# Latent products before context products in a hybrid RWKV-7 / Mamba-2 / MoE layer, with other filler sizes around its scan

## Chip, cores and metric

The kernel runs on one core of one Trainium2 chip. The metric is the device time of one execution in microseconds (us). Runs of one kernel are summed up by their median. A second, profiled execution gives the trace from which rows are read here.

## What is computed

One trunk layer over 512 latent tokens and 256 context tokens of width 1024, in float32. All projections of the mixer come from one input matrix; both token streams go through it:

```python
pc = jnp.einsum('bld,de->ble', hc, p['w_in'])      # context, 256 rows
pl = jnp.einsum('bld,de->ble', hl, p['w_in'])      # latent, 512 rows
ya_c, ya_l = rwkv_branch(rw_c, rw_l, p, ctx_out)   # RWKV-7, two directions
yb_c, yb_l = ssm_branch(ss_c, ss_l, p, rows, ctx_out)   # Mamba-2, two directions
out_l = merge(ya_l, yb_l, gt_l, p)
...
def step(s, inp):                                  # RWKV: the state is carried from token to token
    sa = jnp.einsum('bhvk,bhk->bhv', s, -kk_t)
    s = s * w_t[:, :, None, :] + sa[..., None] * (kk_t * a_t)[:, :, None, :] + v_t[..., None] * k_t[:, :, None, :]
...
xbc = jax.nn.silu(dw_conv_centred(xbc, p['ssm_conv_w'], p['ssm_conv_b']))   # Mamba: convolution over 5 tokens
```

A mixture of 16 experts follows. The change does not touch it.

## The kernel before

**Stages.** The trace has these stretches, in us from the start of the span: normalisation and first projections up to 165; the preparation of the RWKV scan (`rw_all`) up to some 640; the RWKV scan in four passes up to 1141; the Mamba stage (`ssd_prep`, `ssd_main`) up to 1500; then the merge, the routing and the experts.

**A projected block.** `inproj_g` (L301) makes 128 output columns of `w_in`: eight k-tiles (`KT`), each with three products, since a float32 number is split into a rounded part and its rest: `whi`·`hlH`, `whi`·`hlL`, `wlo`·`hlH`. That is 24 matmuls of 512 columns into the PSUM tile `pl` for the latents (L312) and, where `ctx` holds, 24 of 256 columns into `pc` for the context (L315). The two alternate, matmul by matmul, so that both end together. The function is a generator: it yields the columns of each matmul. Both tiles come from the PSUM pool `ip` under one tag, with 4 buffers in `rw_all`, 3 in the scan and 2 in the Mamba stage (`ipb`). The weights are loaded (`wraw`), rounded by ScalarE (`whi`, L284) and subtracted by GpSimd (`wlo`, L287) a block ahead.

**Who takes the results away.** In the scan, blocks are the Mamba convolution's (`conv`, L445). ScalarE copies `pc` (L453) and `pl` (L454) into `u`, VectorE does four multiply-adds (L463), GpSimd a product (L466). Blocks of the kinds z and g (`zgate`, L471) have no context. In `rw_all`, `shift` (L319) reads `pl` and `pc`: ScalarE copies, VectorE does two multiply-adds each.

**The scan and its filler.** `scan` (L895) has 12 steps a pass, 48 in all. A step is a chain: small matmuls (`pch<-SV,sAL`), a VectorE copy to `R` (L930), small matmuls (`pch<-R,sTT`), copies to `SV` by VectorE (L944) and ScalarE (L945), small matmuls (`pch<-SV,sBT`), and a VectorE product into the next `SV` (L954). While TensorE would wait for each of the three, `self.feed(self.hop)` issues matmuls of projected blocks worth `HOP` = 3200 columns (L940, L948, L960). The sum of filler is fixed: what isn't issued in the scan is issued after it.

**After the scan.** The readout of the last pass, `rw_out` (L963), treats two heads' pairs one after the other. Each has three products into one PSUM tile `po` (a single buffer): means (L981), variances (L987) and gate (L996), with ScalarE and VectorE work between them. The loop at L2027 issues one part of it, then 3000 columns of filler, eight times; then the rest of the filler is issued (L2030). Next come 36000 columns of gate blocks (L2043, kind g), which TensorE's order places partly among the products of the readout, and the first transposes of the Mamba stage (`sps<-ident,Bc`, L1134), whose operands `Bc`, `Cc`, `xc` SyncE's queue loads (L1119 to L1124).

**Order.** On TensorE the order within a stage is that of the code. On the other engines a scheduler sets it.

Of the kernel before, what the change touches and what calls it, by code (L numbers as in the profile page):

```python
# [19 lines left out]
SEQ = 512  # L20
CTX = 256
TOK = CTX + SEQ
KT = D // 128
# [1 line left out]
ROWS = SEQ // NCOL  # L25
EPS = 1e-6

HOP = 3200
HOP3 = 2600
HOP4 = 8000  # L30
PREPC = 7500
# [56 lines left out]
class Block:  # L88
# [212 lines left out]
    def inproj_g(self, n, ctx, w):  # L301


        nc = self.nc
        hi, lo = w
        pl = self.ip.tile([128, SEQ], F32, name="pl", tag="ip", bufs=self.ipb)
        pc = self.ip.tile([128, CTX], F32, name="pc", tag="ip", bufs=self.ipb) if ctx else None
        for j, (w_, H) in enumerate(((hi, 0), (hi, 1), (lo, 0))):
            x = (self.hlL, self.hcL) if H else (self.hlH, self.hcH)
            for kt in range(KT):  # L310
                e = dict(start=j + kt == 0, stop=j == 2 and kt == KT - 1)
                nc.tensor.matmul(pl[:n], w_[:, kt, :n], x[0][:, kt, :], **e)  # L312
                yield SEQ
                if ctx:
                    nc.tensor.matmul(pc[:n], w_[:, kt, :n], x[1][:, kt, :], **e)  # L315
                    yield CTX
        return pl, pc

    def shift(self, dst, off, pl, pc, blk):  # L319
# [1626 lines left out]
def body(tc, A, out):  # L1946
    with ExitStack() as ctx:
        B = Block(tc, A, out)
# [22 lines left out]
        pl = lambda n, **k: tc.tile_pool(name=n, bufs=1, reuse_waits="tile", **k)  # L1971
# [4 lines left out]
        with ExitStack() as hx:  # L1976
# [22 lines left out]
            with pl("ip", space=PSUM) as B.ip, pl("sc") as sc, pl("scp", space=PSUM) as scp, ExitStack() as scx:  # L1999
                B.zeros(sc)  # L2000
                B.setup_conv(sc, ("u", "acc", "sg"))
                B.fill, B.credit = B.filler(sc, B.blocks), 0
                B.hop = HOP
                side = B.rw_last(scp)
                with tc.manual_schedule(engines={mybir.EngineType.PE}):
                    for p in range(4):
                        py = B.scan(sc, scp, p, side)
                        if p == 0:
                            for _ in side:
                                B.feed(SF)  # L2010
                            tpx.close()
                            rs = rsx.enter_context(pl("rs", side="right"))
                            B.sqs, B.ones = rs.tile([128, SEQ], F32, name="sqs"), rs.tile([128, 128], F32, name="ones")
                            sp = hx.enter_context(pl("ssdc", side="right"))
                            sc2 = scx.enter_context(pl("sc2"))
                            B.late = itertools.chain(B.ada_late(sc2, 0), B.ada_late(sc2, 1))
                        side = B.rw_out(sc2, scp, p, py)
                        next(side)
                        if p == 1:
                            setup = B.ssd_setup(sp, sc2, scp)  # L2020
                            next(setup)
                            next(setup)
                        elif p == 2:
                            next(setup)
                            next(setup)
                            next(setup, None)
                    for _ in range(8):  # L2027
                        next(side, None)
                        B.feed(3000)
                    B.feed(1 << 30)  # L2030
                    B.fill = B.filler(None, [("g", b) for b in range(G1, 16)])
                    next(B.fill)
# [75 lines left out]
```

## Time and profile before

| | us |
|---|---|
| median of three runs | 2183.39 (2180.47 to 2185.78) |
| the profiled execution | 2184.98 |
| its span from first to last instruction | 2183.1 |
| TensorE busy in it | 1923.5 (88%) |
| VectorE, ScalarE, GpSimd busy | 1171.0, 847.5, 634.0 |

A matmul's duration in the trace holds its way through the array, and successive matmuls overlap: the time that a matmul costs in a row of them is the distance of starts, not the duration. Idle time of an engine counts only where something later waits for that engine.

### The profile page before, as it was taken

How to read it: one execution, taken by the hardware profiler on the slowest of the kernel's cores; microseconds unless marked ns; L12 is line 12 of the kernel's file. 1: busy time of each engine (PE TensorE's matmuls, PEld its weight loads, DVE VectorE, ACT ScalarE, POOL GpSimd, SP SyncE). 2: the span in 40 equal slices, each digit the busy share in tenths (PEclk: the TensorE clock that was granted, in tenths of full speed). 3: DMA queues.
4: the chain of work that ended last, by engine and by line, in shares of the span. 5: the costliest groups of instructions: out<-in, count | busy, mean ns of one | idle time of the engine just before them, and what ended most of it. 6: DMA issues, size and time to landing. Idle time of an engine off the chain costs nothing. (4 is left out here: it accounts for less than half of the span.)

```text
span 2183.1 us, 35294 instructions
## 1 busy us (share of the span) xinstructions
PE 1923.5 (88%) x13996; PEld 1270.6 (58%) x14016; DVE 1171.0 (54%) x1941; ACT 847.5 (39%) x1423; POOL 634.0 (29%) x482
## 2 busy tenths in 40 slices
PE   4979798889768887999997999789999998999997
PEld 2756566566646665666775665467887453433332
DVE  4455987887895858444542466763455112322214
ACT  5444454455343344352535443454333121111113
POOL 2243333433241222332334475663111000000002
PEclk8989998898888999999999999989999999999999
DMA  6246679768879686886546334336866898999997
GB/s 234 77 110 152 158 162 196 146 169 178 183 180 244 184 255 211 286 260 192 162 125 209 113 112 143 131 132 233 279 219 265 334 369 328 409 409 409 408 409 300
DMA packets 444735, 495.16 MB, mean 227 GB/s; under 512 B 138521, under 2 KB 339471, under 8 KB 441499
## 3 DMA queue, kind: packets, MB, share of 16 engines
q1 hardware_dynamic: 419899, 449.29, 64.9%
q0 software_dynamic: 7808, 26.74, 3.4%
q10 hardware_dynamic: 16864, 16.88, 2.4%
q8 instruction: 110, 1.80, 0.3%
q14 instruction: 54, 0.44, 0.1%
HBM read 393.96 MB, written 97.98 MB: 225 GB/s over the span
## 5 line engine op out<-in xcount | busy, mean ns | idle before, releaser
L287 POOL TENSOR_TENSOR wlo<-wraw,whi 128x1024 fp32r<-128x1024 f32 x92 | 231.1, 2512 | 483.0 <-ACT whi L284 222.0
L312 PE MATMUL pl<-hlH,whi 128*128 128x512 f32 x672 | 243.1, 440 | 20.8 <-ACT zg L484 6.5
L312 PE MATMUL pl<-hlH,wlo 128*128 128x512 f32 x672 | 237.8, 431 | 0.0
L312 PE MATMUL pl<-hlL,whi 128*128 128x512 f32 x672 | 232.7, 426 | 0.0
L1705 PE MATMUL ph<-ew,xe 128*64 128x512 f32 x432 | 197.2, 599 | 2.0 <-DMA ew<-in_exp_w_dram 2.0
L1704 PE MATMUL ph<-ew,xe 128*64 128x512 f32 x432 | 196.9, 598 | 0.0
L284 ACT ACTIVATE whi<-wraw 128x1024 fp32r<-128x1024 f32 x93 | 98.1, 1055 | 220.8 <-DMA wraw<-in_w_in_dram 133.4
L312 PEld LDWEIGHTS pl<-hlH,whi 128*128 128x128 f32 x672 | 131.0, 199 | 64.4 <-issue 15.5
L312 PEld LDWEIGHTS pl<-hlL,whi 128*128 128x128 f32 x672 | 127.3, 194 | 39.9 <-issue 14.1
L312 PEld LDWEIGHTS pl<-hlH,wlo 128*128 128x128 f32 x672 | 127.8, 196 | 38.0 <-issue 13.1
L1704 PEld LDWEIGHTS ph<-ew,xe 128*64 128x64 f32 x432 | 56.6, 137 | 110.8 <-issue 109.8
L463 DVE SCALAR_TENSOR_TENSOR cacc<-u,cst,cacc 128x772 f32<-128x772 f32 (+1 forms) x96 | 97.9, 1020 | 30.9 <-ACT cacc L459 29.3
L315 PE MATMUL pc<-hcH,whi 128*128 128x256 f32 (+1 forms) x312 | 97.1, 312 | 12.8 <-ACT u L454 7.4
L1791 PE MATMUL pye<-ew,ewx 128*64 128x512 f32 x448 | 107.7, 632 | 0.0
L315 PE MATMUL pc<-hcH,wlo 128*128 128x256 f32 (+1 forms) x312 | 96.6, 313 | 0.0
L315 PE MATMUL pc<-hcL,whi 128*128 128x256 f32 (+1 forms) x312 | 95.6, 310 | 0.0
L1214 ACT ACTIVATE M<-sel,ncumT 128x128 f32<-128x128 f32 x256 | 69.1, 386 | 66.3 <-PE sel L1211 66.2
L1711 ACT ACTIVATE ewx<-ph 128x512 f32<-128x512 f32 x30 | 17.9, 598 | 187.3 <-PE ph L1705 173.8
L1819 DVE TENSOR_TENSOR macc<-macc,psc 128x512 f32<-128x512 f32 x56 | 37.7, 685 | 93.2 <-PE psc L1814 93.1
L466 POOL TENSOR_TENSOR cacc<-cacc,csg 128x772 f32<-128x772 f32 (+1 forms) x24 | 42.9, 1788 | 146.4 <-ACT csg L465 145.8
L1215 DVE TENSOR_TENSOR M<-M,cb 128x512 f32<-128x512 f32 x64 | 63.0, 996 | 34.6 <-ACT M L1214 34.5
L1870 POOL TENSOR_TENSOR macc<-macc,x 128x512 f32<-128x512 f32 x7 | 11.4, 1653 | 227.8 <-DVE macc L1869 226.5
(575 smaller groups left out, 4265.7 us busy)
## 6 DMA issues: line engine op xcount, KB each, us to landing
ew<-in_exp_w_dram SPq DMA_DIRECT2D x126, 1024.0 KB
ew<-in_exp_w_dram SPq DMA_DIRECT2D x90, 512.0 KB
wraw<-in_w_in_dram SPq DMA_DIRECT2D x83, 512.0 KB
adaw<-in_ada_w_dram SPq DMA_DIRECT2D x24, 1024.0 KB
cst<-in_exp_w_dram SPq DMA_DIRECT2D x14, 1024.0 KB
BTd<-BT ACTq DMA_DIRECT2D x48, 256.0 KB
sAL<-ALd SPq DMA_DIRECT2D x23, 512.0 KB
sBT<-BTd SPq DMA_DIRECT2D x23, 512.0 KB
```

Of the source, the lines that this page charges most:

```text
L284: pin(nc.scalar.activation(hi, raw, AF.Copy))
L287: self.lo.tensor_sub(lo, raw, hi.bitcast(F32))
L312: nc.tensor.matmul(pl[:n], w_[:, kt, :n], x[0][:, kt, :], **e)
L315: nc.tensor.matmul(pc[:n], w_[:, kt, :n], x[1][:, kt, :], **e)
L463: e.scalar_tensor_tensor(acc[:, s0:s0 + n0], u[:, s0 + k:s0 + k + n0], cw[:, b, k:k + 1], acc[:, s0:s0 + n0], op0=OP.mult, op1=OP.add)
L466: nc.gpsimd.tensor_mul(acc[:, s:s + n], acc[:, s:s + n], sg[:, s:s + n])
L1214: nc.scalar.activation(M[:, c], pt[:, c * 128:c * 128 + 128], AF.Exp, bias=self.ncumT[:, c, r:r + 1])
L1215: nc.vector.tensor_mul(M.rearrange("p c t -> p (c t)"), M.rearrange("p c t -> p (c t)"), cb)
L1704: nc.tensor.matmul(ph[e][f][0:64], x, w1[j][:, fs], start=kt == 0, stop=kt == 7, skip_group_check=True)
L1705: nc.tensor.matmul(ph[e][f][64:128], x, w3[j][:, fs], start=kt == 0, stop=kt == 7, skip_group_check=True)
L1791: nc.tensor.matmul(py[64 * c:64 * c + 64], hd[e][:, kt], w2[j][:, 512 * c:512 * c + 512], start=kt == 0, stop=kt == 7, skip_group_check=True)
L1819: nc.vector.tensor_add(a, a, pc)
```

## The change

Three edits. In `inproj_g`, all 24 latent matmuls of a block now come first, then its 24 context matmuls; the weights, the operands and the count stay. `HOP` falls from 3200 to 3000 columns. The loop after the scan feeds 8000 columns a step in place of 3000.

```diff
-HOP = 3200
+HOP = 3000
...
-        for j, (w_, H) in enumerate(((hi, 0), (hi, 1), (lo, 0))):
-            x = (self.hlL, self.hcL) if H else (self.hlH, self.hcH)
-            for kt in range(KT):
-                e = dict(start=j + kt == 0, stop=j == 2 and kt == KT - 1)
-                nc.tensor.matmul(pl[:n], w_[:, kt, :n], x[0][:, kt, :], **e)
-                yield SEQ
-                if ctx:
-                    nc.tensor.matmul(pc[:n], w_[:, kt, :n], x[1][:, kt, :], **e)
-                    yield CTX
+        for o, x, cols in ((pl, (self.hlH, self.hlL), SEQ), (pc, (self.hcH, self.hcL), CTX))[:1 + ctx]:
+            for j, (w_, h) in enumerate(((hi, 0), (hi, 1), (lo, 0))):
+                for kt in range(KT):
+                    nc.tensor.matmul(o[:n], w_[:, kt, :n], x[h][:, kt, :], start=j + kt == 0, stop=j == 2 and kt == KT - 1)
+                    yield cols
         return pl, pc
...
                     for _ in range(8):
                         next(side, None)
-                        B.feed(3000)
+                        B.feed(8000)
                     B.feed(1 << 30)
```

**Where one block ends and the next begins, in the scan.** TensorE's order in the last pass, before the change; `hl` are latent operands, `hc` context operands, and `whi` follows `wlo` where the next block begins:

```order
L315 MATMUL pc<-hcH,wlo 128x256
L312 MATMUL pl<-hlH,wlo 128x512
L315 MATMUL pc<-hcH,wlo 128x256
L312 MATMUL pl<-hlH,whi 128x512
L315 MATMUL pc<-hcH,whi 128x256
```

The same place now:

```order
L311 MATMUL pc<-hcH,wlo 128x256 x2
L311 MATMUL pl<-hlH,whi 128x512 x5
L898 MATMUL pch<-R,sTT 64x64 x8
L311 MATMUL pl<-hlH,whi 128x512 x3
L311 MATMUL pl<-hlL,whi 128x512 x3
```

The first context matmul of a block stood second in it, and now stands after its 24 latent ones.

**ScalarE at the end of the scan, before.** `u` is the convolution's input, `oy` the scan's result, `SV` a copy of the chain:

```order
L454 ACTIVATE u_6507<-pl 128x8x64
L453 ACTIVATE u_6507<-pc 128x256
L459 ACTIVATE cacc<-u_6507,cst 128x772
L945 ACTIVATE SV<-pch 64x2x128
L971 ACTIVATE oy<-py_10402 128x512
L971 ACTIVATE oy<-py_10400 128x512
```

And now:

```order
L450 ACTIVATE u_6509<-pl 128x8x64
L941 ACTIVATE SV<-pch 64x2x128
L967 ACTIVATE oy<-py_10318 128x512
L967 ACTIVATE oy<-py_10316 128x512
L284 ACTIVATE whi<-wraw 128x1024
L449 ACTIVATE u_6509<-pc 128x256
L455 ACTIVATE cacc<-u_6509,cst 128x772
```

The copy of `pl` stood directly ahead of that of `pc`; now four instructions lie between.

**TensorE after the scan, before.** From the last context matmul of the filler to the gate product of the second pair; the rows between are gate blocks:

```order
L315 MATMUL pc<-hcH,wlo 128x256
L996 MATMUL po<-cst,lg 128x512
L312 MATMUL pl<-hlH,whi 128x512 x8
L312 MATMUL pl<-hlL,whi 128x512 x8
L312 MATMUL pl<-hlH,wlo 128x512 x8
L312 MATMUL pl<-hlH,whi 128x512 x8
L312 MATMUL pl<-hlL,whi 128x512 x4
L981 MATMUL po<-oy,cst 128x512
L312 MATMUL pl<-hlL,whi 128x512 x4
L312 MATMUL pl<-hlH,wlo 128x512 x8
L987 MATMUL po<-oy,cst 128x512
L996 MATMUL po<-cst,lg 128x512
```

The second pair's three products now:

```order
L977 MATMUL po<-oy,cst 128x512
L311 MATMUL pc<-hcH,whi 128x256 x7
L311 MATMUL pc<-hcL,whi 128x256 x8
L311 MATMUL pc<-hcH,wlo 128x256 x8
L983 MATMUL po<-oy,cst 128x512
L311 MATMUL pl<-hlH,whi 128x512 x8
L311 MATMUL pl<-hlL,whi 128x512 x8
L311 MATMUL pl<-hlH,wlo 128x512 x8
L311 MATMUL pl<-hlH,whi 128x512 x2
L992 MATMUL po<-cst,lg 128x512
L311 MATMUL pl<-hlH,whi 128x512 x6
```

The filler reached to the first pair's gate product and now reaches to the second pair's variances; 26 matmuls of gate blocks stand between the second pair's last two products, where there were none. From the last small matmul of the scan to the first transpose of `Bc` there are 28416 columns more than before.

## Rows read from the trace of the kernel before

**Rows 1.** The page: busy time, share of the span, instructions.

```profile
PE 1923.5 (88%) x13996; PEld 1270.6 (58%) x14016; DVE 1171.0 (54%) x1941; ACT 847.5 (39%) x1423; POOL 634.0 (29%) x482
```

**Rows 2.** By stretch: length; busy PE, PEld, DVE, ACT, POOL; granted clock; DMA; GB/s.

```profile
165.00:703.00 538.00, 446.76 (x3810) 335.13 (x3808) 422.05 (x760) 251.99 (x372) 192.94 (x117) 0.89 0.76 175
703.00:826.90 123.90, 108.05 (x1489) 81.39 (x1489) 90.12 (x164) 45.74 (x69) 35.08 (x28) 0.98 0.77 228
...
1054.80:1140.90 86.10, 83.74 (x1002) 63.73 (x1002) 43.06 (x68) 40.62 (x53) 31.95 (x24) 1.00 0.52 156
1140.90:1182.50 41.60, 30.49 (x117) 21.97 (x117) 13.02 (x14) 22.71 (x27) 16.78 (x13) 0.88 0.54 186
```

**Rows 3.** What TensorE waited for, 703 to 1140.9 us: total, times, longest.

```profile
PE pch L902 <- DVE SV L944: 10.4, 9, 2.8
PE pc L315 <- ACT u L454: 7.4, 9, 1.0
PE pl L312 <- ACT u L454: 5.4, 5, 1.1
PE pch L902 <- DVE SV L954: 4.6, 4, 3.6
PE pch L902 <- ACT SV L945: 3.1, 6, 1.2
PE pch L902 <- DVE R L930: 2.9, 3, 2.2
```

**Rows 4.** Instructions in order of time at one block boundary in the last pass.

```profile
1117.71 0.42 DVE L930 COPY R<-pch 128x256 f32<-128x256 f32 x1 [1.85 <-PE pch L902]
...
1119.05 1.11 ACT L454 ACTIVATE u<-pl 128x512 f32<-128x512 f32 x1 [4.36 <-PE pl L312]
...
1120.21 0.39 PE L315 MATMUL pc<-hcH,whi 128*128 128x256 f32 x1 [0.85 <-ACT u L454]
...
1121.23 0.68 PE L902 MATMUL pch<-R,sTT 64*64 64x64 f32 x16
```

**Rows 5.** Line L315 alone: minimum, median, maximum in ns of one instruction.

```profile
L315 PEld LDWEIGHTS pc<-hcH,wlo x312: 134/189/337, 68.5 to 1148.5; 128*128 128x128 f32 x152, 128*64 128x64 f32 x4
L315 PE MATMUL pc<-hcH,wlo x312: 274/280/686, 68.6 to 1148.7; 128*128 128x256 f32 x152, 128*64 128x256 f32 x4
```

**Rows 6.** TensorE in order of time, in the first projections.

```profile
68.58 0.99 PE L315 MATMUL pc<-hcH,wlo 128*128 128x256 f32 x7
```

**Rows 7.** TensorE in order of time, after the scan.

```profile
1146.49 1.12 PE L987 MATMUL po<-oy,cst 128*128 128x512 f32 x2 [0.29 <-ACT oy L984]
...
1151.64 2.12 PE L312 MATMUL pl<-hlH,whi 128*128 128x512 f32 x8 [1.76 <-ACT u L453]
1153.60 1.99 PE L312 MATMUL pl<-hlL,whi 128*128 128x512 f32 x8
1155.42 1.98 PE L312 MATMUL pl<-hlH,wlo 128*128 128x512 f32 x8
...
1168.07 1.13 PE L996 MATMUL po<-cst,lg 128*128 128x512 f32 x2 [3.47 <-ACT osd L989]
1174.79 3.78 PE L312 MATMUL pl<-hlH,whi 128*128 128x512 f32 x8 [5.59 <-ACT zg L484]
...
1182.47 0.60 PE L1134 MATMUL sps<-ident,Bc 128*128 128x128 f32 x4
```

**Rows 8.** The same stretch on VectorE: the reading of the first gate product.

```profile
1155.65 0.67 DVE L997 TENSOR_TENSOR od<-od,po 128x512 f32<-128x512 f32 x1
```

**Rows 9.** The columns of rows 2, around the last of these waits.

```profile
1172.00:1177.00 5.00, 2.21 (x5) 1.82 (x6) 1.38 (x2) 1.11 (x2) 1.42 (x2) 0.50 1.01 369
```

**Rows 10.** SyncE's queue: the first loads of the Mamba stage.

```profile
1168.93 0.52 SPq L1119 DMA_DIRECT2D Bc<-xd  x1
```

**Rows 11.** What TensorE waited for, 165 to 703 us.

```profile
PE pbt L760 <- DVE X L741: 21.3, 12, 4.8
PE pvt L621 <- DVE v L329: 6.8, 4, 3.1
```

## Prediction

> **What bounds the kernel now.** The page comes first: TensorE is busy for 88% of the span, the next engine for 54% [rows 1]. That is a mean, so the second view is the busy time by stretch [rows 2]. In the scan's last pass (1054.8 to 1140.9) TensorE is busy for 83.7 of 86.1 us: the scan's chain of waits is covered there, and a column of filler taken out shortens the pass. In 703 to 826.9 it is 108.1 of 123.9 us while VectorE has 90.1: there the chain sometimes ends last. Right after the scan (1140.9 to 1182.5) TensorE has only 30.5 of 41.6 us, at a mean granted clock of 0.88: too little filler is left. Before 703 (`rw_all`) VectorE leads with 422.1 of 538 us, and TensorE waits.
>
> The third view is what TensorE waited for in 703 to 1140.9 [rows 3]. Two kinds must be told apart. The waits of `pch` (10.4 + 4.6 + 3.1 + 2.9 us, 22 times) belong to the scan's chain. Those of `pc` and `pl` on ScalarE's copy `u` (7.4 + 5.4 us, 14 times) belong to the filler, and their place in time [rows 4] shows why. With three PSUM buffers, `pl` and `pc` of one block hold two, the next block's `pl` takes the third, and its `pc` needs the buffer of the `pl` that has just ended. That `pl` is copied from 1119.05 on, 1.11 us long; the `pc` matmul, second in its block, stands idle for 0.85 us and starts at 1120.21.
>
> **The change part by part: the order of products.** Nothing is added or removed: each block keeps its 24 matmuls of either size and their weight loads. Once the context products come last, `pl` has been complete for 24 matmuls when its buffer is wanted, and the next block's `pl` takes a buffer that was copied a block earlier. Seven context matmuls in a row took 0.99 us [rows 6]; with the 0.28 us of one (the median of [rows 5]) that is (0.99 - 0.28) / 6 = 0.118 us from start to start, so 24 last 2.8 us against the copy's 1.11 us. All 14 waits should go: 12.8 us. What is late next? After the example the chain's next matmul starts at 1121.23, and its `R` was ready at 1117.71 + 0.42 = 1118.13 [rows 4]: 3.1 us of room. Where a chain wait follows more closely the gain is swallowed; I take off 2 us: **-10.8 us** (bounds 0, if a chain wait takes the place of each, and -15, as 0.85 us idle in the example is 1.0 us of lost starts). The copies of `pc` now end a block alone, behind other ScalarE work, which costs nothing as long as `u` has its second buffer.
>
> Does TensorE pay for the new order? Before, a latent and a context matmul with the same weights stood side by side. The row says that nothing was shared: each of 312 context matmuls of a kind has a weight load of its own, 0.189 us at the median, and at 0.118 us from start to start it is hidden even where context follows context [rows 5, 6]. I take 0. The Trainium skill, page "TensorE: Matmul & The Clock Gate", section "Part 2: What happens when you issue a matmul", speaks against the change: weights stay put, so load once and multiply repeatedly, and a load takes the columns divided by 1.2, some 107 ns for 128. By that page the change would give up a shared load for 3 x 312 = 936 matmuls, an estimate of 100 us; by the rows it gives up none.
>
> **HOP.** 46 of the 48 steps lie after 703, but all 48 get three times 200 columns less: 28800 columns. Eight latent matmuls start 1.82 us apart (1153.60 to 1155.42, [rows 7]), 0.2275 us for 512 columns, so 28800 columns are 12.8 us. An interval that now ends in a chain wait gives nothing back: 22 of 46 x 3 = 138, or 16%. **-10.7 us** (bounds 0 and -12.8). Fewer convolution blocks in the scan also take VectorE work out of it, which I don't count.
>
> **After the scan.** The 28416 columns of the new order come here: **+12.6 us**. They lie between the readout's products, and cover what is idle now [rows 7]: 0.29 us before the variances, 1.76 us on the copy of `pc`, 3.47 us on `osd`, 5.59 us on `zg`: **-11.1 us**. Before the last product runs TensorE waits 3.47 us and after it 5.59 us, and the granted clock then is 0.50 [rows 9], the lower level of 1.2 GHz: eight matmuls in 3.78 us. The 23 matmuls from 1174.79 to the transposes at 1182.47 took 7.7 us, at 0.2275 us each they take 5.2: **-2.4 us** if TensorE stays busy. New waits: the second pair's means need the single `po` buffer, which is free when VectorE has read the gate product, 1155.65 + 0.67 - 1146.49 = 9.8 us after the first pair's variances start [rows 7, 8]. In the new order two feeds (8000 columns, 3.55 us each) and two products (1.1 us each) lie between, 9.3 us, and one more rounding of weights stands in ScalarE's order ahead of that reading. I take **+3 us** of waits (bounds 0 and 8). They also hold the loads of `Bc` and `xc`: issued 13.5 us before the transposes now [rows 7, 10], one weight load earlier in SyncE's order after the change, with 45 gate-block matmuls (10.2 us) behind the last product to cover them. Sum for this stretch: +2.1 us.
>
> **`rw_all` and the rest.** `HOP` isn't used there. The order is, and it lets `shift` begin on `pl` 2.8 us earlier; VectorE's order changes with it. I take 0 between -9 and +8 (below).
>
> **Sum.** -10.8 - 10.7 + 2.1 = -19.4 us on the profiled execution's 2184.98: 2165.6. The median lies 1.6 us lower (2183.39), so I forecast **2164**.
>
> **The rivals.**
> 1. *The scan is bound by its chain.* Then neither the filler's cut nor the buffer's release shortens it, and the columns are paid for after it: +2.1 us, about 2185.5. For it: 22 chain waits, VectorE at 73% in 703 to 826.9. Against: the last pass, 97% TensorE [rows 2], and the room of 3.1 us [rows 4].
> 2. *Weight loads come to light (slower).* If a context matmul hides only 0.118 us of its 0.189 us load once 24 stand in a row, each loses 0.07 us: 936 x 0.07 = 66 us, less the gain of 19: about 2230. It decides from 0.02 us a matmul on (19.4 / 936). Against it: the seven in a row at 0.118 us. The section of the Trainium skill named above would put the loss higher still, at its estimate of 100 us.
> 3. *`rw_all` gains too.* TensorE waits 21.3 us for `X` and 6.8 us for `v` on VectorE [rows 11]. If `shift` moves out of their way and a third of it goes, 9 us: 2155.
> 4. *`rw_all` loses.* VectorE executes in order; an early `shift` that waits for its `pl` holds up the products behind it. If each of the 12 waits for `X` grows by one VectorE instruction of 512 columns, 0.67 us as in [rows 8], that is +8: 2172.
> 5. *The edits do nothing to the waits* (the scheduler moves the copies so that the buffer is late again): only `HOP` counts, -8.6: 2175.
>
> **How the numbers follow.** Likeliest 0.60, with its own range 2157 to 2171; rival 1: 0.08; 2: 0.03; 3: 0.12; 4: 0.11; 5: 0.06. The measurement tells about 0.2% (4.4 us) from no change: faster is below 2179.0. Faster: 0.60 + 0.12 + 0.11 + 0.06 less a tail of 0.03, 0.86; same: 0.08 (rival 1 and some of the tail); slower: 0.06 (rival 2, the rest). The range takes in rivals 3, 4 and 5 and the bounds of new waits: 2150 to 2179.
>
> **What the new profile would show.** Right: no waits of projected blocks' products for `u` in the scan; a last pass shorter by some 3 us; the stretch from the scan's last matmul to the first `Bc` transpose about as long as now (41.6 us), but with TensorE busy for nearly all of it at a granted clock near 1. Wrong: chain waits well over 21 us; context matmuls over 0.118 us from start to start; a wait of more than 5 us between the second pair's products or before the `Bc` transposes; a change before 703.

## The result and the profile after

The changed kernel takes **2206.5 us** (median of 4 runs, 2201.4 to 2207.1) against 2184.6 (4 runs, 2180.5 to 2189.1): a recorded ratio of 1.0092, 95% interval 1.0074 to 1.0110 (the quotient of the two medians is 1.0100). It is slower; the forecast was 2164 in 2150 to 2179. The profiled execution took 2201.42 us, span 2199.3.

The page of after: busy time, share of the span, instructions (to be set against [rows 1]).

```profile
PE 1928.4 (88%) x14016; PEld 1273.5 (58%) x14016; DVE 1166.6 (53%) x1941; ACT 851.3 (39%) x1424; POOL 629.7 (29%) x482
```

No engine was given more work, so the time went into waits and clock. What TensorE waited for in the scan of after (engine, line, releaser: total us, times, longest), to be set against [rows 3]:

```profile
PE pch L898 <- DVE SV L940: 16.1, 8, 7.2
PE px L832 <- DMA T<-d: 6.1, 1, 6.1
PE pch L898 <- DVE R L926: 5.3, 6, 1.5
PE pch L898 <- ACT SV L941: 4.3, 7, 1.5
PE py L898 <- DVE SV L940: 3.9, 1, 3.9
PE pch L898 <- DVE SV L950: 3.8, 5, 1.3
```

The waits of `pl` and `pc` for `u` are gone, as forecast. The chain's waits have grown from 21.0 us (the four rows of `pch` in [rows 3]) to 29.5 (the four rows of `pch` here).

After by stretch, columns as in [rows 2]: the last pass over the same steps, and the stretch from the scan's end to the first transpose of `Bc`.

```profile
1056.50:1140.10 83.60, 81.37 (x990) 61.34 (x989) 40.85 (x65) 39.92 (x52) 29.16 (x23) 1.00 0.52 162
1140.10:1196.20 56.10, 43.61 (x196) 34.22 (x196) 23.28 (x20) 29.46 (x36) 24.78 (x18) 0.88 0.41 136
```

The last pass is 2.5 us shorter (forecast 3). The stretch after the scan takes 56.1 us in place of 41.6, at the same granted clock of 0.88, so the idle time that the new columns were to cover is still there: 56.1 - 43.6 = 12.5 us without TensorE, 41.6 - 30.5 = 11.1 before. Where it sits now, TensorE in order of time:

```profile
1162.77 2.08 PE L977 MATMUL po<-oy,cst 128*128 128x512 f32 x2 [4.13 <-DVE od L993]
...
1189.00 3.78 PE L311 MATMUL pl<-hlH,whi 128*128 128x512 f32 x8 [8.36 <-ACT zg L480]
```

The first wait is the one for the single `po`, and its cause is on VectorE: the reading of the gate product stands behind four multiply-adds of the convolution.

```profile
1156.95 5.16 DVE L459 SCALAR_TENSOR_TENSOR cacc<-u,cst,cacc 128x772 f32<-128x772 f32 x4
1162.03 0.68 DVE L993 TENSOR_TENSOR od<-od,po 128x512 f32<-128x512 f32 x1
```

The second is a chain over several engines. The rows of ScalarE, GpSimd and SyncE's queue in after, in order of time:

```profile
1170.68 12.58 SPq L281 DMA_DIRECT2D wraw<-in_w_in_dram  x2
...
1177.30 0.86 ACT L461 ACTIVATE csg<-cacc 128x772 f32<-128x772 f32 x1 [0.92 <-DVE cacc L459]
...
1178.23 1.89 POOL L462 TENSOR_TENSOR cacc<-cacc,csg 128x772 f32<-128x772 f32 x1 [1.79 <-ACT csg L461]
1180.05 2.81 POOL L287 TENSOR_TENSOR wlo<-wraw,whi 128x1024 fp32r<-128x1024 f32 x1
...
1183.36 0.52 SPq L1115 DMA_DIRECT2D Bc<-xd  x1
...
1187.41 1.06 ACT L284 ACTIVATE whi<-wraw 128x1024 fp32r<-128x1024 f32 x1 [7.79 <-DMA wraw<-in_w_in_dram]
1188.37 0.58 ACT L480 ACTIVATE zg<-pl 128x512 f32<-128x512 f32 x1
```

GpSimd makes the last convolution's product at 1178.23, then `wlo`; the second of the two weight loads is issued only when `wlo` has freed a buffer (1182.9), ScalarE's `whi` waits for it until 1187.41, and `zg`, a copy that was ready to run since TensorE ended that block, stands behind `whi`. Eight matmuls after the wait take 3.78 us, the lower of the clock's two levels, as in [rows 7].

### The profile page after: what moved, and what is told of

It reads as the page before. It is cut to its first block, busy times and chain, and to the rows that moved or that the text cites. A ratio compares the mean times of both kernels' runs of the same rounds, so it can differ in the third digit from the quotient of the medians.

```text
span 2199.3 us, 35321 instructions
## 1 busy us (share of the span) xinstructions
PE 1928.4 (88%) x14016; PEld 1273.5 (58%) x14016; DVE 1166.6 (53%) x1941; ACT 851.3 (39%) x1424; POOL 629.7 (29%) x482
## 5 line engine op out<-in xcount | busy, mean ns | idle before, releaser
L287 POOL TENSOR_TENSOR wlo<-wraw,whi 128x1024 fp32r<-128x1024 f32 x92 | 223.2, 2426 | 507.5 <-ACT whi L284 301.7
L311 PE MATMUL pl<-hlH,whi 128*128 128x512 f32 x672 | 217.1, 443 | 17.6 <-ACT zg L480 8.4
L311 PE MATMUL pl<-hlL,whi 128*128 128x512 f32 x672 | 213.0, 437 | 0.0
L311 PE MATMUL pl<-hlH,wlo 128*128 128x512 f32 x672 | 209.1, 431 | 0.0
L311 PEld LDWEIGHTS pl<-hlH,whi 128*128 128x128 f32 x672 | 126.4, 198 | 57.4 <-issue 16.6
L311 PEld LDWEIGHTS pl<-hlH,wlo 128*128 128x128 f32 x672 | 123.6, 194 | 42.4 <-issue 17.0
L459 DVE SCALAR_TENSOR_TENSOR cacc<-u,cst,cacc 128x772 f32<-128x772 f32 (+1 forms) x96 | 105.0, 1094 | 28.2 <-ACT cacc L455 26.6
L1700 PEld LDWEIGHTS ph<-ew,xe 128*64 128x64 f32 x432 | 56.5, 137 | 109.0 <-issue 107.9
L1787 PE MATMUL pye<-ew,ewx 128*64 128x512 f32 x448 | 110.9, 647 | 0.0
L1815 DVE TENSOR_TENSOR macc<-macc,psc 128x512 f32<-128x512 f32 x56 | 37.7, 685 | 89.5 <-PE psc L1810 89.3
L1866 POOL TENSOR_TENSOR macc<-macc,x 128x512 f32<-128x512 f32 x7 | 11.4, 1654 | 229.7 <-DVE macc L1865 228.4
L1787 PEld LDWEIGHTS pye<-ew,ewx 128*64 128x64 f32 x448 | 33.2, 149 | 65.3 <-issue 64.6
L1803 DVE TENSOR_TENSOR yhl<-yf,yhl 64x512 fp32r<-64x512 f32 x30 | 20.5, 686 | 84.0 <-ACT yhl L1802 83.5
L690 POOL TENSOR_TENSOR t<-nkk,a 128x768 f32<-128x768 f32 x16 | 39.1, 2443 | 87.2 <-ACT a L659 59.3
```

The source lines that it names most:

```text
L287: self.lo.tensor_sub(lo, raw, hi.bitcast(F32))
L311: nc.tensor.matmul(o[:n], w_[:, kt, :n], x[h][:, kt, :], start=j + kt == 0, stop=j == 2 and kt == KT - 1)
L459: e.scalar_tensor_tensor(acc[:, s0:s0 + n0], u[:, s0 + k:s0 + k + n0], cw[:, b, k:k + 1], acc[:, s0:s0 + n0], op0=OP.mult, op1=OP.add)
L690: nc.gpsimd.tensor_mul(ka, nkk, a)
L1700: nc.tensor.matmul(ph[e][f][0:64], x, w1[j][:, fs], start=kt == 0, stop=kt == 7, skip_group_check=True)
L1787: nc.tensor.matmul(py[64 * c:64 * c + 64], hd[e][:, kt], w2[j][:, 512 * c:512 * c + 512], start=kt == 0, stop=kt == 7, skip_group_check=True)
```

## The experiments

All were timed in five rounds, in four groups, each on one chip beside the kernel before (medians of before 2188.6, 2186.4, 2186.8, 2185.3 us). The table cuts each profiled execution at the same instructions. Preparation: from the first pair's transposes (`pvt`) to the scan's first matmul. Start: to the zeroing of the first `py` (step 3). Passes: from one zeroing to the next, the last to its last `py<-sRB`. Tail: to the first transpose of `Bc`. Mamba: to the merge's first product. Lengths in us; one execution each, so a few us between kernels mean little.

| kernel | prep. | start | pass 1 | 2 | 3 | 4 | tail | Mamba | ratio to before [95%] |
|---|---|---|---|---|---|---|---|---|---|
| before | 562.6 | 39.5 | 122.2 | 110.9 | 115.1 | 77.2 | 41.5 | 331.3 | |
| after | 573.5 | 36.4 | 125.9 | 111.1 | 106.3 | 75.7 | 56.1 | 330.7 | 1.0092 [1.0074, 1.0110] |
| 1 order | 581.7 | 35.6 | 132.9 | 112.5 | 106.8 | 76.6 | 41.8 | 329.2 | 1.0061 [1.0037, 1.0085] |
| 2 HOP | 559.7 | 37.5 | 138.4 | 97.9 | 112.3 | 76.2 | 63.9 | 331.6 | 1.0096 [1.0063, 1.0129] |
| 3 feed | 563.0 | 38.2 | 123.0 | 113.3 | 113.0 | 77.1 | 47.8 | 331.9 | 1.0025 [1.0006, 1.0045] |
| 4 HOP, feed | 559.2 | 37.6 | 138.5 | 97.6 | 112.3 | 76.1 | 60.9 | 330.4 | 1.0096 [1.0064, 1.0128] |
| 5 order in prep. | 579.3 | 37.3 | 128.8 | 111.7 | 115.5 | 77.4 | 41.6 | 331.2 | 1.0082 [1.0056, 1.0108] |
| 6 order in scan | 565.9 | 35.5 | 129.7 | 114.8 | 105.2 | 76.8 | 41.1 | 334.4 | 0.9992 [0.9973, 1.0011] |
| 7 HOP late | 554.0 | 37.9 | 126.4 | 112.4 | 109.8 | 81.0 | 49.5 | 331.0 | 1.0061 [1.0038, 1.0085] |
| 8 after, zg on DVE | 580.1 | 32.9 | 130.2 | 113.9 | 107.9 | 75.7 | 48.8 | 341.8 | 1.0115 [1.0095, 1.0136] |
| 9 as 5, VT on DVE | 581.2 | 44.8 | 121.2 | 112.1 | 114.7 | 77.6 | 41.5 | 330.2 | 1.0061 [1.0039, 1.0082] |
| 10 as 5, not pair 8 | 572.5 | 42.3 | 121.2 | 112.5 | 115.4 | 77.4 | 41.8 | 331.0 | 1.0070 [1.0048, 1.0092] |
| 11 as 6, zg repaired | 554.2 | 36.5 | 128.9 | 112.5 | 105.2 | 76.8 | 43.0 | 325.7 | 0.9960 [0.9939, 0.9981] |
| 12 after, zg repaired | 571.3 | 33.0 | 132.9 | 111.9 | 107.7 | 75.7 | 50.0 | 333.7 | 1.0049 [1.0032, 1.0066] |
| 13 prep. by weight | 567.1 | 37.7 | 123.6 | 111.7 | 114.4 | 77.3 | 41.5 | 331.1 | 1.0028 [1.0006, 1.0050] |
| 14 before, zg repaired | 565.4 | 37.9 | 122.2 | 111.6 | 112.9 | 77.4 | 41.7 | 327.4 | 0.9970 [0.9954, 0.9985] |
| 15 HOP, zg repaired | 561.4 | 37.4 | 136.8 | 98.6 | 110.9 | 76.3 | 55.8 | 335.7 | 1.0070 [1.0048, 1.0093] |
| 16 as 11, by weight | 559.1 | 37.9 | 122.9 | 114.7 | 103.3 | 77.5 | 42.6 | 328.2 | 0.9957 [0.9941, 0.9974] |

**1 to 4: the edits apart.** One hunk of the diff each: the order of products (1), `HOP = 3000` (2), `B.feed(8000)` (3), the last two together (4).

> Latent products first, alone (HOP 3200 and feeds of 3000 as before). Theory A (the loss is made after the scan, by the columns that HOP and the 8000 put there): the stretch from the scan's last matmul to the first Bc transpose stays within 3 us of the 42.6 us of before, the waits of pl and pc for the copy u in the scan go, and the time is 8 to 12 us under the kernel before. Theory B (the order of products upsets VectorE and ScalarE in the preparation and the first pass): 5 to 13 us over the kernel before, with 5 to 8 us of it ahead of 703 us.

> HOP 3000 alone, the old order of products, feeds of 3000. Theory A: the scan is shorter by some 10 us and the stretch after it longer by 10 to 14 us, so the time is within 5 us of the kernel before. Theory B: nothing ahead of 703 us changes, the stretch after the scan takes the columns into its waits, and the time is 5 to 10 us under the kernel before.

> Feeds of 8000 columns alone. The old order leaves some 12000 columns after the scan, so two feeds take them all. Theory A: the first pair's means come up to 2.5 us later and the time is within 4 us of the kernel before. Theory B: no difference, within 4 us.

> HOP 3000 and feeds of 8000, the old order of products. Theory A: the waits of the changed kernel after the scan are here too (4 us ahead of the second pair's means, 8 us ahead of the third gate block), the stretch after the scan is 52 to 57 us, and the time is 2 to 6 us over the kernel before. Theory B: the stretch after the scan is 42 to 46 us and the time 6 to 10 us under the kernel before.

No edit gains by itself. 2, 3 and 4 are slower than either theory expected (by 21, 5 and 21 us over before), and 1 lies at or just over the upper end of theory B's range; by place, theories A (the tail) and B (the preparation and first pass) each hold a part. The order loses ahead of the tail; `HOP` loses 22 us in the tail and gives nothing in the scan (the passes sum to 425.4 before, 424.8 with it); 8000 columns lose 6 us in the tail. They do not add up: 0.6% and 1.0% apart, 0.9% together.

**5 and 6: where the order loses.** `inproj_g` takes the new loop in one stage and the old one elsewhere:

```diff
+        if self.ipb == 4:        # 5: the preparation; 6: ipb == 3, the scan
+            for o, x, cols in ((pl, ...
+        else:
+            for j, (w_, H) in enumerate(...
```

> The new order of products in the preparation of the scan alone; the scan's filler and what follows keep the old order, HOP 3200 and 3000 columns a step. Theory B (the order's loss is made in the preparation, where ScalarE copies r ahead of the weights' rounding and of VT, so that TensorE waits for VT, falls to the lower granted clock and hands a later start to the scan): the scan begins 8 to 18 us later than before, 1.004 to 1.008 times the time before (about 2198). Rival (the loss is made by the order in the scan's first pass): the scan begins within 3 us of before and the time is within 0.2%.

> The new order in the scan's filler alone; preparation in the old order, HOP 3200, 3000 columns a step. Theory B: the waits of projected blocks for u in the scan go (12.8 us in the trace of before) and nothing is lost ahead of it, so 5 to 12 us faster, 0.994 to 0.998 times the time before. Rival (the first pass loses by the order itself, as the run with the order alone lost 10.7 us there): first pass 5 to 11 us longer, time within 0.2% of before or above.

The loss is made in the preparation: 579.3 us, and in the five kernels with the new order as it is there 571 to 582 (mean 577), against 554 to 566 (mean 560) in the ten that keep the old one. In 5 the first pass is 6.6 us longer as well, though its order is the old one; 9 and 10, below, don't show that. In the scan alone (6) the order neither loses nor gains, where 5 to 12 us were expected: the rival came out, a first pass longer by 7.5 us. The scan's waits in 6:

```profile
PE pch L909 <- DVE SV L951: 15.9, 12, 5.2
PE pch L909 <- DVE R L937: 7.3, 7, 3.2
PE pch L909 <- ACT SV L952: 3.5, 6, 1.3
PE px L843 <- DMA T<-d: 3.4, 2, 2.9
PE pch L909 <- DVE SV L961: 2.1, 3, 1.3
```

12.8 us of waits for `u` are gone, and the chain's four rows of `pch` come to 28.8 us in place of 21.0 [rows 3]: 8 of 13 us are taken back by the chain. By place, the third pass is 9.9 us shorter and the first two 11.4 longer.

**7: HOP's cut in the last two passes only.**

```diff
+                        B.hop = HOP if p < 2 else 3000
                         py = B.scan(sc, scp, p, side)
```

> HOP 3200 in the first two passes and 3000 in the last two; order and the rest as before. Theory H (HOP's cut shortens a pass where TensorE is the bound, and in the first pass it only lets VectorE's dt work in ahead of the chain's copies): the first two passes within 3 us of before, the last two 3 to 6 us shorter together, the stretch after the scan 8 to 12 us longer for 14400 columns (6.4 us) and new waits: 1.001 to 1.004 times the time before. Rival (the columns are covered after the scan): that stretch at most 3 us longer, time 0.998 to 1.000.

The second pass moved by 1.5 us and the first by 4.2 (at most 3 expected), and 14400 columns cost the tail 8 us, as theory H has it; but the last two passes together gave 1.4 us in place of 3 to 6, and the ratio is above the expected 1.004. In the last pass VectorE has 42.4 us of work in place of 37.0: again work of its own came to lie elsewhere.

**8, 12, 14, 15: the wait for `zg`.** In 8 VectorE copies the first two gate blocks after the scan; the others have two `zg` buffers in the Mamba stage as well ("repaired").

```diff
-            nc.scalar.activation(t, pl, AF.Copy)
+            nc.vector.tensor_copy(t, pl) if G1 <= b - 16 < G1 + 2 else nc.scalar.activation(t, pl, AF.Copy)
...
-        t = pool.tile([128, SEQ], F32, name="zg", tag=tag, bufs=bufs)
+        t = pool.tile([128, SEQ], F32, name="zg", tag=tag, bufs=bufs or (2 if self.ipb == 2 else 1))
```

> The changed kernel, but VectorE in place of ScalarE copies the first two gate blocks after the scan (zg), so that the copy doesn't stand behind a rounding of weights. Theory C (after the scan TensorE waits 8.4 us, and then runs at the lower clock, because zg stands behind whi, which waits for a weight load): that wait goes, the stretch from the scan's end to the first Bc transpose falls from 56 to 47 to 50 us, the time from 1.009 to 1.005 to 1.006 times that of before. Rival (the loads of Bc, issued 12.8 us before the transposes, end just as late): the transposes wait for them instead, the stretch stays above 53 us and the time at 1.008 to 1.010.

The tail fell to 48.8 us, as theory C said, and the time did not fall (1.0115, where 1.005 to 1.006 was expected): the wait came back one block later, since the second copy needs the one `zg` buffer, whose store is queued behind the loads of `Bc` and `xc`. TensorE's waits in 8, from the scan's last steps into the Mamba stage:

```profile
PE pl L311 <- DVE zg L480: 8.3, 2, 7.5
PE po L977 <- DVE od L993: 4.1, 1, 4.1
```

The same view of 12, from the scan's end on:

```profile
PE po L977 <- DVE od L993: 4.1, 1, 4.1
PE sps L1136 <- DMA xc<-xd: 3.4, 4, 1.5
PE sps L1130 <- DMA Bc<-xd: 1.9, 1, 1.9
PE pl L311 <- DVE zg L480: 0.7, 1, 0.7
```

> The changed kernel with the same two repairs of zg. Theory C2: the 8.4 us wait before the transposes and the 7.5 us wait one block later, which took its place when VectorE copied zg into a single buffer, both go; the stretch from the scan's end to the first Bc transpose takes 47 to 50 us and the Mamba stage stays at 331: 1.003 to 1.006 times the time before. Rival: the loads behind it end last instead, 1.008 or more.

With two buffers both waits go, as theory C2 has it, and the changed kernel comes from 1.0092 to 1.0049. By the traces the tail gets 6.0 us shorter and the Mamba stage 3.0 longer. What ends next is there: 5.3 us for `xc` and `Bc`.

> The kernel before with only the two repairs of zg (VectorE copies the first two gate blocks after the scan; two zg buffers in the Mamba stage). If the repair made the 0.4% of the run with the scan's new order: 0.996 to 0.998. If the order made it: 0.999 to 1.001.

> HOP 3000 alone, old order, with the two repairs of zg; HOP 3000 alone was 1.0096. Theory H (the scan gives back 4 us at most for 28800 columns, and 12.6 us of them are paid after it): the repairs take off 0.3 to 0.5%, 1.0045 to 1.0065 stays. Rival (HOP fails by the waits for zg after the scan alone): 1.001 or less.

The repair gains 0.3% on the kernel before as well (14), so that little of the 0.43% in 12 is peculiar to the new tail. With it the cut of `HOP` still costs 1.0% (1.0070 of 15 over 0.9970 of 14), more than theory H expected: the passes give back 1.4 us (422.6 against 424.0), the tail takes 14.1 more, of which the columns are 12.6, and the Mamba stage 8.3. In 15 TensorE doesn't wait for `zg` in the tail at all, so `HOP`'s loss is not that wait.

**9, 10, 13: how the preparation loses.** From 5 on, 9 lets VectorE copy `VT` in the last of the eight pairs, and 10 keeps the old order in that pair; 13 sorts the products by weight part (16 latent, 16 context ones with `whi`, then 8 and 8 with `wlo`).

```diff
-            nc.scalar.activation(VT[:, i0:i0 + n], pt[:, :n], AF.Copy)
+            (nc.vector.tensor_copy(VT[:, i0:i0 + n], pt[:, :n]) if p == 7 else nc.scalar.activation(...))
```

> The new order in the preparation alone, as in the run of that (1.0082), and in the last of its eight pairs VectorE in place of ScalarE copies VT, so that VT no longer stands behind whi. In that run the last pair took 83.2 us and the scan began at 690.5. Theory V (the last pair's loss is VT standing behind a rounding of weights on ScalarE, with the lower granted clock after that wait): the last pair takes 76 to 78 us, the time is 1.004 to 1.006 times that of before. Rival (the loss is made by other work, VectorE's above all): the last pair stays at 81 us or more and the time at 1.007 or more.

> The new order in the first seven pairs of the preparation, the old one in the last pair and in all that follows; ScalarE's order around the last VT is that of before. Theory V: the last pair takes 73 to 76 us as in the kernels with the old order, and what is left is the 6 to 9 us of the first three pairs: 1.003 to 1.005 times the time before. Rival (the loss is one of the state at the start of the pair, such as VectorE running late): the last pair still takes 80 us or more, time 1.007 or more.

> In the preparation alone the products are sorted by weight part: 16 latent and 16 context products with whi, then 8 and 8 with wlo; whi is released after two thirds of a block, as before, and pl ends 8 context products (0.94 us) ahead of pc in place of 24. The rest as before. Theory W (the new order loses in the preparation because whi is held to the end of the context products, some 1.9 us longer): the preparation up to the scan's start takes within 5 us of before (676), time 1.000 to 1.003 times that of before. Rival (the early end of the latents reorders ScalarE and VectorE; the last VT still stands behind whi here): scan from 684 on, 1.005 to 1.008.

The last pair (from its `pvt` to the scan) takes 73.6 us before, 81.2 in after and 83.2 in 5; 79.0 in 9, 77.0 in 10, 75.5 in 13. ScalarE in order of time at its start, in the kernel before:

```profile
604.40 0.40 ACT L791 ACTIVATE Tf<-T 96x256 f32<-96x256 f32 x1
604.70 0.84 ACT L622 ACTIVATE VT<-pvt 128x512 f32<-128x512 f32 x2
606.22 1.06 ACT L284 ACTIVATE whi<-wraw 128x1024 fp32r<-128x1024 f32 x1 [0.67 <-DMA wraw<-in_w_in_dram]
```

The same place in after:

```profile
603.01 0.67 ACT L323 ACTIVATE r<-pl,cst 128x512 f32<-128x512 f32 x1
607.47 1.06 ACT L284 ACTIVATE whi<-wraw 128x1024 fp32r<-128x1024 f32 x1 [3.80 <-DMA wraw<-in_w_in_dram]
608.43 0.85 ACT L618 ACTIVATE VT<-pvt 128x512 f32<-128x512 f32 x2
```

`VT` now stands behind a `whi` that waits 3.80 us for its load. TensorE, in order of time, waits for `VT` and then runs at the lower of the clock's levels:

```profile
609.06 0.65 PE L652 MATMUL ra<-low,lwh 128*128 128x512 f32 x1 [2.25 <-ACT VT L618]
```

The last pair, and 20 us in it, in the view by stretch of before:

```profile
602.51:676.08 73.57, 55.46 (x544) 39.47 (x542) 71.14 (x140) 33.04 (x50) 25.79 (x16) 0.86 0.81 196
606.00:626.00 20.00, 17.59 (x123) 11.72 (x121) 19.09 (x29) 13.90 (x17) 12.36 (x7) 1.00 0.59 135
```

The same two stretches of after:

```profile
603.52:684.74 81.22, 61.66 (x545) 42.75 (x543) 71.68 (x139) 33.13 (x49) 26.02 (x16) 0.79 0.74 177
606.00:626.00 20.00, 17.75 (x105) 11.48 (x104) 15.98 (x23) 13.43 (x17) 7.15 (x4) 0.74 0.45 106
```

The same matmuls (544, 545) keep TensorE busy for 6.2 us more: most of the pair's 7.6 us is clock, and the clock falls behind a wait of 2 us. The other runs agree: in after, 1, 5, 8 and 12 TensorE waits 2.25 to 2.44 us for `VT` at this place and the granted clock falls to 0.50; in before, 9 and 13 it waits 0.44 to 1.22 us and the clock stays at 1.00 for the next 15 us and more. (In 10, at 1.78 us, it falls for some 4 us, behind a further wait.) No run changes this wait alone. 10 shows the place: with ScalarE's order of before the pair is 6 us shorter than in 5. 9 shows the mechanism in part (79.0 us against 76 to 78 expected): the clock holds behind `VT`, and falls 20 us later, behind a wait of 2.79 us for `X`.

But the ratios, 1.0061 and 1.0070, are hardly under the 1.0082 of 5, and 10's preparation is still 12 us over the mean of the old order: more than half of the loss lies in the seven pairs ahead. There, too, the waits for `VT` grow. What TensorE waited for between 165 and 680 us, the rows of `VT`, before:

```profile
PE ra L656 <- ACT VT L622: 6.5, 5, 2.2
PE rac L632 <- ACT VT L622: 3.2, 2, 2.7
```

The same in after:

```profile
PE rac L628 <- ACT VT L618: 12.0, 3, 4.3
PE ra L652 <- ACT VT L618: 4.0, 3, 2.3
```

Over the whole preparation these waits come to 14 to 20 us in the five kernels with the new order and to 6 to 10 in the ten with the old one; those for `X` are 24 to 28 and 26 to 31. In the mean TensorE is idle for 104 us in the five and 91 in the ten, and busy for 473 and 470: over the whole preparation some 14 of the 17 us are waits, 8 of them for `VT`, and the clock is the smaller part. ScalarE at the fifth pair of after shows the order seen above, and TensorE's wait behind it is 4.31 us:

```profile
387.18 1.06 ACT L284 ACTIVATE whi<-wraw 128x1024 fp32r<-128x1024 f32 x1 [2.40 <-DMA wraw<-in_w_in_dram]
388.14 0.85 ACT L618 ACTIVATE VT<-pvt 128x512 f32<-128x512 f32 x2
```

13 takes most of the loss back (567.1 us), and its waits for `VT` are 5.3 us. In the new order `whi` is needed until 16 of the context products have run, 40 of a block's 48 matmuls in place of 32; in 13 it is 32 again. In 13 `VT` still stands behind `whi`, but the load is there 1.96 us into the wait in place of 3.80. That speaks for theory W. It isn't proved by it, since 13 also ends `pl` later than the new order does. A rival that no run tests lies in SyncE's queue, which issues the weight loads: between 165 and 680 us its store of `zg` waits 51.0 us for VectorE in after and 20.5 before, and loads queue up behind it. Against it: that wait is still 42.9 us in 13.

**11 and 16: the faster kernels.** 11 is 6 with the repair of `zg`; 16 sorts the scan's products by weight part.

> The kernel before with the new order in the scan's filler alone (0.9992 by itself), the first two gate blocks after the scan copied by VectorE, and two zg buffers in the Mamba stage. Theory C2 (TensorE's wait for zg after the scan is one of ScalarE's order and of the single zg buffer, whose store is held in SyncE's queue): the 5.6 us wait goes and does not come back one block later, the granted clock stays up: 5 to 10 us faster, 0.994 to 0.998 times the time before. Rival (the Mamba stage waits as long for Bc or for the next weights): 0.998 to 1.001.

> As the faster kernel (new order in the scan's filler alone, zg repaired; 0.996), but in the scan the products are sorted by weight part, so that whi is released as in the old order and pl still ends 0.94 us ahead of pc. If whi's longer hold costs in the scan's first pass: 0.992 to 0.995. If not: 0.995 to 0.998.

Both beat both kernels, by 0.4% over before. Most of it is the repair (14: 0.3%), though not in the expected way: TensorE still waits 5.5 us for `zg` in the tail of 11, now behind the readout's work on VectorE; it is the Mamba stage that is 3 to 6 us shorter in 11, 14 and 16, by one execution each, and why, no run shows. Between 11 and 16 there is no difference that these intervals show.

## Why the prediction was wrong

The spans of the two profiled executions differ by 16.2 us: preparation +10.9, start -3.1, the four passes -6.4, tail +14.5, Mamba stage -0.6, the rest elsewhere. Forecast were 0 for the preparation, -21.5 for the scan and +2.1 for the tail.

- **"-10.8 us" for the order's stalls: the mechanism was right, the size wrong.** The 14 waits went. "I take off 2 us", for chain waits that follow closely, should have been 8: the chain's waits grew from 21.0 to 28.8 us in 6, and the time by the recorded ratio is -1.7 us (0.9992 of 2186.4; interval -5.9 to +2.4). The room of 3.1 us [rows 4] was read from one place in the last pass; the first two passes, where VectorE is busier, got 11.4 us longer in 6.
- **"-10.7 us" for `HOP`: the step that failed in the scan.** It priced columns as if the rest of the scan stood still, and left VectorE uncounted. With 3000 columns and the old order of products the first pass takes 138.4 us (15: 136.8) and the second 97.9: VectorE's order, which a scheduler sets, ends the Mamba stage's `dt` work in the first pass, where it ended in the second before. The first pass by stretch, in the kernel before:

```profile
715.60:837.80 122.20, 104.59 (x1350) 77.26 (x1351) 93.07 (x162) 44.97 (x64) 37.26 (x31) 1.00 0.73 221
```

  The same pass in 2:

```profile
712.20:850.60 138.40, 110.29 (x1337) 81.51 (x1338) 104.84 (x184) 46.21 (x66) 33.43 (x27) 0.88 0.66 193
```

  VectorE in 2 in order of time, at two places of that pass:

```profile
795.96 4.93 DVE L1048 RECIPROCAL dt<-dt 64x768 f32<-64x768 f32 x1
800.82 0.35 DVE L944 COPY SV<-pch 64x256 f32<-64x256 f32 x1
...
826.37 6.32 DVE L1069 TENSOR_TENSOR_SCAN dt<-dt,dt 32x512 f32<-32x512 f32 x6
832.71 0.42 DVE L930 COPY R<-pch 128x256 f32<-128x256 f32 x1
```

  The last of these `dt` rows in the kernel before, 8 us into its second pass:

```profile
845.94 7.20 DVE L1069 TENSOR_TENSOR_SCAN dt<-dt,dt 32x512 f32<-32x512 f32 x6
```

  The chain's `SV` and `R` stand behind such rows; the granted clock of the pass falls from 1.00 to 0.88. Of the 16.2 us that the first pass loses the second gives back 13.0. That the order of `dt` makes this was read from the rows; no run moved `dt` alone. In the changed kernel itself these six rows stay in the second pass (from 852.88 on), so this path isn't its own. Its passes sum to 419.0 us, and those of 8 and 12, with the same order and `HOP`, to 427.7 and 428.2, against 425.4 before and 428.8 in 1: of the 21.5 us forecast for the scan nothing is left in the mean. Why the cut gives so little in the new order stays open.
- **"+2.1 us" after the scan: +14.5 in after.** The +12.6 of columns held; "-11.1" of covered waits and "-2.4" of clock did not come. The step that failed took the columns as cover: they bring convolution blocks with them, whose multiply-adds (VectorE), products (GpSimd) and roundings (ScalarE) stand in order ahead of the readout and of `zg`. The wait for `po`, forecast as "+3 us", was 4.13; the "45 gate-block matmuls" behind the last product stopped at the third block, since two `pl` buffers wait for `zg`. With the wait for `zg` repaired (12) the tail is still 8.5 us longer than before; the wait for `po` is still there, 4.1 us.
- **"0" for `rw_all`: +17 us** (means of the preparation, 577 against 560; the ratio of 5 is 1.0082). Rival 4 had the sign, with half the size and another path: the waits for `X` did not grow, those for `VT`, behind the weights' chain on ScalarE, did, and the clock adds the smaller part. Taking 0 for a stage in which the order of two engines changes was the largest error of a single term.
- Rival 2, loads that come to light, falls: eight context matmuls in a row take 1.11 us in after (at 1148.31), (1.11 - 0.28) / 7 = 0.119 from start to start, as priced. The Trainium skill (page "TensorE: Matmul & The Clock Gate", section "Part 2: What happens when you issue a matmul") says that weights that stay put can be loaded once and used for many matmuls. Of the 100 us that the prediction estimated by that page nothing is seen in this row either.
- Of the signs named beforehand, a wait over 5 us before the transposes (8.36), chain waits over 21 us (29.5), and a change before 703 all came.

## What to carry to other kernels

Moving matmuls is not only a matter of columns: each block brings its copies, multiply-adds and weight roundings to engines that execute in order, and there it stands ahead of work that TensorE waits for. So read, for the new place, what is queued behind each of those instructions before the columns are counted as cover. Where a buffer is read by two groups of products, putting all of one group last holds it longer (here for 40 of 48 matmuls in place of 32); and a repaired wait should be followed one link further, since the next buffer of the same chain may hold it just as long.

## What was not expected of the hardware

A wait of 2.25 us in the preparation of after was followed by a fall of the granted clock: 0.74 between 606 and 626 us where it was 1.00 before the change, matmuls of 512 columns at 0.65 us in place of 0.39, and 6.2 us more of TensorE time in the pair. The length of a wait alone doesn't tell, though: in the kernel before, TensorE waited 2.75 us for `VT` at 239.38 and 2.24 us at 460.38, and the clock stayed at 1.00 for the next 20 us. The kernel before itself spread over 2173.5 to 2199.9 us in 21 runs on one chip, 1.2%, so that differences of 0.3% here rest on 6 to 29 runs each.
